# Loading and splitting weight blocks in pairs in a float32 gMLP and dilated-attention kernel

## The chip, the cores and the metric

The kernel runs on one core of a Trainium2 chip. The metric is the device time of one execution in microseconds (us), the median over several runs. The engines are called as in the profile: PE (TensorE matmul), PEld (its weight loads), DVE (VectorE), ACT (ScalarE), POOL (GpSimd) and SP (SyncE, which here issues the DMA transfers, one after the other, in the order of its program).

## What is computed

The reference is a two-layer decoder on 2048 tokens of width 1024, all in float32. Cut to its products:

```python
def gmlp_layer(x, c, ada_w, ada_b, norm_g, w_in, sgu_g, w_s, b_s, w_out):
    shift, scale, gate = ada_mod(c, ada_w, ada_b, 3)
    h = rms_norm(x, norm_g) * (1 + scale) + shift
    u, v, z = jnp.split(h @ w_in, 3, axis=-1)            # 3 x 2048 columns
    v = rms_norm(jax.nn.gelu(v), sgu_g)                  # chunks of 128 tokens, 8 groups
    mixed = einsum('gts,bcsge->bctge', tril(w_s), v) + b_s
    return x + gate * ((gelu(u) * mixed * silu(z)) @ w_out)

def shared_kv(...):        # h @ w_kv, 1536 columns; k is normalised per head
def dilated_layer(...):
    q, z = split(h @ w_in) # 3 groups of 8 heads x 128, and z with 1024 columns
    o = softmax-merge over 3 groups of banded, dilated attention(q, k, v)
    return x + gate * ((o * silu(z)) @ w_out)
```

## The kernel before

The 2048 tokens are worked on in four quarters Q = 0 to 3 of 512 tokens. In each quarter the dense products follow one another on PE: v (`dense`), u and z of the first layer (`dense_f`), its output o (`dense`), then k and v of the shared attention (kv, `dense`), and the blocks q02, q01, q00 and z0b (`dense_s`; in quarter Q the blocks q(Q)2, q(Q)1, q(Q)0, z(Q)b). The last stage, `finish`, merges the attention and multiplies by the output weights (tiles `wo`).

To keep float32 accuracy, each operand is held as a high half, rounded to the matmul type fp32r, and a low half, the remainder. A product is three matmuls: high by high, low by high, high by low. Weights come from DRAM as float32 into a tile `raw_*`; `split` makes the high half by an ACT copy (L242) and the low half by a DVE subtraction (L246), both into a tile `w_*`. The subtraction of the few blocks of `begin` and before is on POOL.

- `wunits` (called by `dense`, `dense_s` and the start, `begin`) loads blocks of 128 rows by 512 columns, 256 KB each: one DMA (L253), one ACT copy, one subtraction. `dense` takes eight such blocks in one pass of 10.9 us of PE. `dense_s` does a 1024x1024 product by seven smaller products of four blocks each (24 matmuls of 128x512 for each half of the tokens); between the products ACT and DVE empty PSUM tiles into sum tiles (`st_*`; L386 adds, L391 copies).
- `dense_f` loads blocks of 2 x 128 rows by 256 columns, 256 KB, four for one block of output columns.
- The raw tiles come from a pool `rp` of six, the `w_*` tiles from a pool `wp` of eight: a load can be issued only when the split has read the tile that it overwrites, and a split only when PE is done with the weights that it overwrites. The tiles `og` (two attention groups' output, 512 KB each) and `zt` of `finish` take places in `wp` too, three a step.
- Beside this chain run generators ("fillers"): attention of the quarter before, preparation of the operands, combined weights, the ada vectors (`aw_*` loads, `acc_*` on DVE). `tick` advances them by a rate at each k of a dense block. In the last z block (quarter 3) these are the generators of `finish`: `w_out` loads the 16 blocks of the output weights (`rawo`; L1055, ACT L1057, POOL L1058), and `first` loads og and zt (L1096, L1098), scales og on ACT (L1105, eight operations) and on DVE (L1043), adds on DVE (L1107) and multiplies by zt on POOL (L1108).
- The query blocks end in a short chain on POOL (L780 to L783), after which SP stores the rows of q (`qd<-st_q..`, L785). The z blocks end in an ACT operation (L791) and a store (`zd<-zb`, L792).

A scheduler orders the instructions of each engine when the program is built. On the chip each engine, and SP's list of transfers, runs in that order: an instruction that waits holds up all that stand behind it on its engine.

Of the kernel before, what the change touches and what calls it, by code (L numbers as in the profile page):

```python
# [12 lines left out]
F32 = mybir.dt.float32  # L13
# [21 lines left out]
def trunk(ctx, tc, out, x, c, a_ada_w, a_ada_b, a_norm_g, a_w_in, a_sgu_g, a_w_spatial,  # L35
# [9 lines left out]

    cp = ctx.enter_context(tc.tile_pool(name="cp", bufs=1))
    big = ctx.enter_context(tc.tile_pool(name="big", bufs=6))
    wp = ctx.enter_context(tc.tile_pool(name="wp", bufs=8))
    rp = ctx.enter_context(tc.tile_pool(name="rp", bufs=6))
    xp = ctx.enter_context(tc.tile_pool(name="xp", bufs=4))  # L50
    ep = ctx.enter_context(tc.tile_pool(name="ep", bufs=6))
    bp = ctx.enter_context(tc.tile_pool(name="bp", bufs=2))
# [194 lines left out]

    def wunits(w, k0, n0, nm, nk=KT, ordered=False):
        us = []
        for kk in range(nk):  # L250
            u = wp.tile([P, 2, 512], F32R, tag="w", name=f"w_{nm}{kk}")
            raw = rp.tile([P, 512], F32, tag="raw", name=f"raw_{nm}{kk}")
            ld = nc.sync.dma_start(raw, w[(k0 + kk) * P:(k0 + kk + 1) * P, n0:n0 + 512])  # L253
            if ordered:
                tc.keep_in_program_order(ld)
            split(u[:, 0, :], u[:, 1, :], raw, ordered)
            us.append(u)
        return us

    last_mm = [None]  # L260
# [24 lines left out]
    def dense_f(hh, hl, w, n0, nm, evac):  # L285

        pts = [pst(f"pd_{nm}_{i}", "d") for i in range(2)]
        for kk in range(0, KT, 4):
            for j in range(0, 4, 2):
                u = wp.tile([P, 2, 2, 256], F32R, tag="w", name=f"w_{nm}{kk + j}")  # L290
                raw = rp.tile([P, 2, 256], F32, tag="raw", name=f"raw_{nm}{kk + j}")
                nc.sync.dma_start(
                    raw, w[(kk + j) * P:(kk + j + 2) * P, n0:n0 + 256].rearrange("(k p) n -> p k n", p=P))
                split(u[:, 0], u[:, 1], raw)
                for k in (kk + j, kk + j + 1):
                    for i in range(2):
                        wh = u[:, 0, k % 2, i * P:(i + 1) * P]
                        wl = u[:, 1, k % 2, i * P:(i + 1) * P]
                        nc.tensor.matmul(pts[i], wh, hh[:, k, :], start=k == 0, stop=False)  # L299
                        nc.tensor.matmul(pts[i], wh, hl[:, k, :], start=False, stop=False)  # L300
                        nc.tensor.matmul(pts[i], wl, hh[:, k, :], start=False, stop=k == KT - 1)  # L301
                    tick(0.25)
        for i in range(2):
            evac(i, pts[i])

# [742 lines left out]
    def finish():  # L1048
        wo = {}

        def w_out(n):
            wh, wl = wo[n] = [big.tile([P, KT, 512], F32R, tag="big", name=f"wo{n}{i}") for i in range(2)]
            for kk in range(KT):
                raw = rp.tile([P, 512], F32, tag="raw", name=f"rawo{n}{kk}")
                nc.sync.dma_start(raw, b_w_out[kk * P:(kk + 1) * P, n * 512:(n + 1) * 512])  # L1055
                yield
                nc.scalar.activation(wh[:, kk, :], raw, AF.Copy)  # L1057
                nc.gpsimd.tensor_tensor(wl[:, kk, :], raw, wh[:, kk, :].bitcast(F32), ALU.subtract)  # L1058
                yield

        gb = [bcast(gd[1:2, n * 512:(n + 1) * 512], f"gb{n}") for n in range(2)]
# [29 lines left out]
        def load(t):  # L1091
            rw = slice(t * P, (t + 1) * P)
            og = {}
            for g in (0, 2):
                og[g] = wp.tile([P, D], F32, tag="w", name=f"og{t}_{g}")
                nc.sync.dma_start(og[g], od[g][rw, :])  # L1096
            og["z"] = wp.tile([P, D], F32, tag="w", name=f"zt{t}")
            nc.sync.dma_start(og["z"], zd[rw, :])  # L1098
            return og

# [140 lines left out]
```

## Time and profile before

| | |
|---|---|
| median of 3 runs | 3061.34 us (3060.43 to 3061.94) |
| profiled execution, span from first to last instruction | 3054.5 us |
| what lies around the span (median less span) | 6.8 us |
| PE busy | 2966.3 us, 97% |
| DVE busy | 2003.8 us, 66% |
| ACT busy | 1632.3 us, 53% |
| POOL busy | 835.4 us, 27% |
| DMA queue | 55% of 16 engines' time, 544.93 MB |

The profile is that of one execution. It has no time of its own besides its span; the runs' times count some microseconds around it. PE is busy nearly all the time, so the table says at once that only the 88.2 us in which PE is idle, and the stretches in which PE runs at its lower clock, can move the time down, and that each wait that is added in front of PE moves it up.

### The profile page before, as it was taken

How to read it: one execution, taken by the hardware profiler on the slowest of the kernel's cores; microseconds unless marked ns; L12 is line 12 of the kernel's file. 1: busy time of each engine (PE TensorE's matmuls, PEld its weight loads, DVE VectorE, ACT ScalarE, POOL GpSimd, SP SyncE). 2: the span in 40 equal slices, each digit the busy share in tenths (PEclk: the TensorE clock that was granted, in tenths of full speed). 3: DMA queues.
4: the chain of work that ended last, by engine and by line, in shares of the span. 5: the costliest groups of instructions: out<-in, count | busy, mean ns of one | idle time of the engine just before them, and what ended most of it. 6: DMA issues, size and time to landing. Idle time of an engine off the chain costs nothing. (4 is left out here: it accounts for less than half of the span.)

```text
span 3054.5 us, 45283 instructions
## 1 busy us (share of the span) xinstructions
PE 2966.3 (97%) x14928; PEld 2487.1 (81%) x14928; DVE 2003.8 (66%) x3550; ACT 1632.3 (53%) x3324; POOL 835.4 (27%) x1112
## 2 busy tenths in 40 slices
PE   5999999999999999999999999999999999999999
PEld 4788888788888778888888878788888888877787
DVE  6777466773567477865577386856676577768862
ACT  4323345666466245566466265566455367867540
POOL 4047113330013023523133033423222131134332
PEclk8999999999999999999999999999999999999999
DMA  7799546663433367753433366743333366778742
GB/s 235 262 296 343 178 152 199 225 227 115 153 97 114 97 201 233 233 189 119 136 101 107 106 194 210 257 152 122 122 108 112 120 192 212 230 252 287 235 153 97
DMA packets 343487, 547.82 MB, mean 179 GB/s; under 512 B 36074, under 2 KB 135628, under 8 KB 343252
## 3 DMA queue, kind: packets, MB, share of 16 engines
q1 hardware_dynamic: 343252, 544.93, 55.1%
q8 instruction: 118, 1.93, 0.3%
q14 instruction: 117, 0.96, 0.1%
HBM read 439.28 MB, written 105.52 MB: 178 GB/s over the span
## 5 line engine op out<-in xcount | busy, mean ns | idle before, releaser
L264 PE MATMUL pd_v<-w_v,hAh 128*128 128x512 f32 x1024 | 328.0, 401 | 1.2 <-ACT hAh L450 1.2
L264 PE MATMUL pd_o<-w_o,yh 128*128 128x512 f32 x1024 | 318.0, 391 | 0.0
L264 PE MATMUL pd_kv<-w_kv,hkh 128*128 128x512 f32 x768 | 241.4, 393 | 3.2 <-DVE w_kv L246 3.2
L264 PEld LDWEIGHTS pd_o<-w_o,yh 128*128 128x128 f32 x1024 | 192.8, 189 | 39.9
L264 PEld LDWEIGHTS pd_v<-w_v,hAh 128*128 128x128 f32 x1024 | 190.1, 192 | 40.2 <-issue 1.7
L933 ACT ACTIVATE pr<-pr,stat,rt 128x256 f32<-128x256 f32 (+1 forms) x320 | 177.4, 556 | 56.6 <-DVE stat L927 39.9
L299 PE MATMUL pd_u<-hAh,w_u 128*128 128x512 f32 x512 | 207.2, 405 | 0.0
L299 PE MATMUL pd_z<-hAh,w_z 128*128 128x512 f32 x512 | 204.8, 400 | 0.0
L301 PE MATMUL pd_u<-hAh,w_u 128*128 128x512 f32 x512 | 201.1, 393 | 2.3 <-DVE w_u L246 2.3
L264 PE MATMUL pd_v<-w_v,hAl 128*128 128x512 f32 x512 | 202.9, 396 | 0.0
L301 PE MATMUL pd_z<-hAh,w_z 128*128 128x512 f32 x512 | 200.5, 392 | 0.0
L264 PE MATMUL pd_o<-w_o,yl 128*128 128x512 f32 x512 | 200.3, 391 | 0.0
L300 PE MATMUL pd_u<-hAl,w_u 128*128 128x512 f32 x512 | 200.3, 391 | 0.0
L300 PE MATMUL pd_z<-hAl,w_z 128*128 128x512 f32 x512 | 199.7, 390 | 0.0
L242 ACT ACTIVATE w_o<-raw_o 128x512 fp32r<-128x512 f32 x128 | 80.0, 630 | 195.0 <-PE pd_o L264 137.3
L246 DVE TENSOR_TENSOR w_o<-raw_o,w_o 128x512 fp32r<-128x512 f32 x128 | 89.9, 704 | 134.1 <-ACT w_o L242 133.4
L264 PEld LDWEIGHTS pd_kv<-w_kv,hkh 128*128 128x128 f32 x768 | 144.1, 189 | 34.9 <-DVE w_kv L246 4.9
L242 ACT ACTIVATE w_u<-raw_u 128x512 fp32r<-128x512 f32 x128 | 79.0, 630 | 164.1 <-PE pd_u L301 70.1
L994 PEld LDWEIGHTS po<-kv,pT 128*128 128x128 f32 x1200 | 147.4, 191 | 14.3 <-POOL pT L968 3.9
L994 PE MATMUL po<-kv,pT 128*128 128x128 f32 x1200 | 150.4, 275 | 5.7 <-POOL pT L968 3.5
L941 POOL TENSOR_TENSOR dg<-pr,ident 128x256 f32<-128x256 f32 x76 | 57.4, 755 | 358.7 <-ACT pr L933 334.4
L242 ACT ACTIVATE w_z<-raw_z 128x512 fp32r<-128x512 f32 x128 | 78.4, 626 | 141.5 <-PE pd_z L301 61.1
(664 smaller groups left out, 7752.3 us busy)
## 6 DMA issues: line engine op xcount, KB each, us to landing
raw_q<-in_b_w_in_dram SPq DMA_DIRECT2D x144, 256.0 KB, 3.8
raw_v<-in_a_w_in_dram SPq DMA_DIRECT2D x128, 256.0 KB, 3.9
raw_u<-in_a_w_in_dram SPq DMA_DIRECT2D x128, 256.0 KB, 3.3
raw_z<-in_a_w_in_dram SPq DMA_DIRECT2D x128, 256.0 KB, 3.1
raw_o<-in_a_w_out_dram SPq DMA_DIRECT2D x128, 256.0 KB, 3.0
qt<-qd SPq DMA_DIRECT2D x96, 260.0 KB, 3.8
raw_kv<-in_w_kv_dram SPq DMA_DIRECT2D x96, 256.0 KB, 3.0
od<-ot SPq DMA_DIRECT2D x96, 256.0 KB, 2.6
```

The source lines that it names most:

```text
L242: nc.scalar.activation(hi, src, AF.Copy)
L246: e.tensor_tensor(lo, src, hi.bitcast(F32), ALU.subtract)
L264: last_mm[0] = nc.tensor.matmul(pt, a, u[:, w, :], start=f, stop=e, skip_group_check=more)
L299: nc.tensor.matmul(pts[i], wh, hh[:, k, :], start=k == 0, stop=False)
L300: nc.tensor.matmul(pts[i], wh, hl[:, k, :], start=False, stop=False)
L301: nc.tensor.matmul(pts[i], wl, hh[:, k, :], start=False, stop=k == KT - 1)
L933: nc.scalar.activation(pr[:, i, :], pr[:, i, :], AF.Exp, bias=mneg[:, i:i + 1], scale=u["rt"][:, h:h + 1], accum_out=lsum[:, i:i + 1])
L941: nc.gpsimd.tensor_tensor(dg, prev, ident.unsqueeze(1).broadcast_to([P, hp, P]), ALU.mult)
L994: nc.tensor.matmul(po[:, h * P:(h + 1) * P], u["pT"][h // hp][:, h % hp, j, :], u["kv"][:, j, kh, 1, :], start=j == 0, stop=j == nk - 1)
```

## The change

Weight blocks are loaded two at a time, in one DMA of 512 KB into one raw tile of 1024 columns, and split by one ACT and one DVE operation of 1024 columns into one `w_*` tile. The pools have half as many tiles of twice the size. In `dense_f` one load takes 4 x 128 rows by 256 columns. In `finish`, `w_out` loads pairs too, but still splits in operations of 512 columns; `og` takes one pair tile of `wp` (both groups in it), and `zt` takes a tile of the raw pool. The matmuls stay as they are.

```diff
-    wp = ctx.enter_context(tc.tile_pool(name="wp", bufs=8))
-    rp = ctx.enter_context(tc.tile_pool(name="rp", bufs=6))
+    wp = ctx.enter_context(tc.tile_pool(name="wp", bufs=4))
+    rp = ctx.enter_context(tc.tile_pool(name="rp", bufs=3))
...
     def wunits(w, k0, n0, nm, nk=KT, ordered=False):
         us = []
-        for kk in range(nk):
-            u = wp.tile([P, 2, 512], F32R, tag="w", name=f"w_{nm}{kk}")
-            raw = rp.tile([P, 512], F32, tag="raw", name=f"raw_{nm}{kk}")
-            ld = nc.sync.dma_start(raw, w[(k0 + kk) * P:(k0 + kk + 1) * P, n0:n0 + 512])
+        for kk in range(0, nk, 2):
+            u = wp.tile([P, 2, 2, 512], F32R, tag="w", name=f"w_{nm}{kk}")
+            raw = rp.tile([P, 2, 512], F32, tag="raw", name=f"raw_{nm}{kk}")
+            ld = nc.sync.dma_start(
+                raw, w[(k0 + kk) * P:(k0 + kk + 2) * P, n0:n0 + 512].rearrange("(k p) n -> p k n", p=P))
             if ordered:
                 tc.keep_in_program_order(ld)
-            split(u[:, 0, :], u[:, 1, :], raw, ordered)
-            us.append(u)
+            split(u[:, 0], u[:, 1], raw, ordered)
+            us += [u[:, :, i, :] for i in range(2)]
         return us
...
-            for j in range(0, 4, 2):
-                u = wp.tile([P, 2, 2, 256], F32R, tag="w", name=f"w_{nm}{kk + j}")
-                raw = rp.tile([P, 2, 256], F32, tag="raw", name=f"raw_{nm}{kk + j}")
-                nc.sync.dma_start(
-                    raw, w[(kk + j) * P:(kk + j + 2) * P, n0:n0 + 256].rearrange("(k p) n -> p k n", p=P))
-                split(u[:, 0], u[:, 1], raw)
...
+            u = wp.tile([P, 2, 4, 256], F32R, tag="w", name=f"w_{nm}{kk}")
+            raw = rp.tile([P, 4, 256], F32, tag="raw", name=f"raw_{nm}{kk}")
+            nc.sync.dma_start(
+                raw, w[kk * P:(kk + 4) * P, n0:n0 + 256].rearrange("(k p) n -> p k n", p=P))
+            split(u[:, 0], u[:, 1], raw)
...
-            for kk in range(KT):
-                raw = rp.tile([P, 512], F32, tag="raw", name=f"rawo{n}{kk}")
-                nc.sync.dma_start(raw, b_w_out[kk * P:(kk + 1) * P, n * 512:(n + 1) * 512])
+            for kk in range(0, KT, 2):
+                raw = rp.tile([P, 2, 512], F32, tag="raw", name=f"rawo{n}{kk}")
+                nc.sync.dma_start(raw, b_w_out[kk * P:(kk + 2) * P, n * 512:(n + 1) * 512]
+                                  .rearrange("(k p) n -> p k n", p=P))
                 yield
-                nc.scalar.activation(wh[:, kk, :], raw, AF.Copy)
-                nc.gpsimd.tensor_tensor(wl[:, kk, :], raw, wh[:, kk, :].bitcast(F32), ALU.subtract)
+                for i in range(2):
+                    k = kk + i
+                    nc.scalar.activation(wh[:, k, :], raw[:, i, :], AF.Copy)
+                    nc.gpsimd.tensor_tensor(wl[:, k, :], raw[:, i, :], wh[:, k, :].bitcast(F32), ALU.subtract)
+                    yield
                 yield
...
-            for g in (0, 2):
-                og[g] = wp.tile([P, D], F32, tag="w", name=f"og{t}_{g}")
+            pair = wp.tile([P, 2, D], F32, tag="w", name=f"og{t}")
+            for i, g in enumerate((0, 2)):
+                og[g] = pair[:, i, :]
                 nc.sync.dma_start(og[g], od[g][rw, :])
-            og["z"] = wp.tile([P, D], F32, tag="w", name=f"zt{t}")
+            og["z"] = rp.tile([P, D], F32, tag="raw", name=f"zt{t}")
```

The scheduler orders the instructions anew. PE's order stays nearly the same; SP has 536 transfers fewer (1980 to 1444), DVE 524 operations fewer (3552 to 3028, the low halves 1048 to 524), ACT 526 fewer (2814 to 2288). Three places matter below.

SP's transfers in the z block of quarter 3, from the time in which its second product (on weights `z3bt`) runs; `raw_z3b` are the weights of the third product, `qd<-st_q30u` the last stores of the query block, `rawo` output weights. Before:

```order
L1055 DMA rawo_25540<-in_b_w_out_dram 128x512
L253 DMA raw_z3b_0_25563<-in_b_w_in_dram 128x512
L253 DMA raw_z3b_1_25568<-in_b_w_in_dram 128x512
L1096 DMA og_0_25554<-od_95 128x1024
L1096 DMA og_2_25556<-od_97 128x1024
L785 DMA qd_92<-st_q30u_24835 128x520
L785 DMA qd_92<-st_q30u_24836 128x520
L1098 DMA zt_25558<-zd 128x1024
L253 DMA raw_z3b_2_25573<-in_b_w_in_dram 128x512
L253 DMA raw_z3b_3_25578<-in_b_w_in_dram 128x512
```

And now, with the loads of the fourth product (`raw_z3bt` from `wt_2`) behind them:

```order
L1055 DMA rawo_22948<-in_b_w_out_dram 128x2x512
L1103 DMA zt_22965<-zd 128x1024
L785 DMA qd_92<-st_q30u_22325 128x520
L1101 DMA og_22962<-od_95 128x1024
L785 DMA qd_92<-st_q30u_22326 128x520
L1101 DMA og_22962<-od_97 128x1024
L253 DMA raw_z3b_0_22970<-in_b_w_in_dram 128x2x512
L253 DMA raw_z3b_2_22975<-in_b_w_in_dram 128x2x512
L253 DMA raw_z3bt_0_23025<-wt_2_117 128x2x512
L253 DMA raw_z3bt_2_23030<-wt_2_117 128x2x512
```

The first two blocks of the third product stood ahead of both og loads and both stores of q; now all of its blocks stand behind these four. Behind these rows come two `rawo` transfers, the two stores of the third product's result (`zd<-zb`) and only then the loads of the fifth product.

DVE at the same place: the low halves of the third product's weights (`w_z3b`), and what stands around them. Before:

```order
L1043 TENSOR_TENSOR og_2_25556<-og_2_25556,wst 128x1024
L246 TENSOR_TENSOR w_z3b_0_25562<-raw_z3b_0_25563,w_z3b_0_25562 128x512
L246 TENSOR_TENSOR w_z3b_1_25567<-raw_z3b_1_25568,w_z3b_1_25567 128x512
L1107 TENSOR_TENSOR og_0_25554<-og_0_25554,og_2_25556 128x1024
L386 TENSOR_TENSOR st_z3bu_25491<-pd_z3ba_25433,st_z3bu_25491 128x512
L386 TENSOR_TENSOR st_z3bu_25492<-pd_z3ba_25434,st_z3bu_25492 128x512
L246 TENSOR_TENSOR w_z3b_2_25572<-raw_z3b_2_25573,w_z3b_2_25572 128x512
```

And now:

```order
L1043 TENSOR_TENSOR og_22962<-og_22962,wst 128x1024
L386 TENSOR_TENSOR st_z3bu_22911<-pd_z3ba_22863,st_z3bu_22911 128x512
L386 TENSOR_TENSOR st_z3bu_22912<-pd_z3ba_22864,st_z3bu_22912 128x512
L1112 TENSOR_TENSOR og_22962<-og_22962 128x1024
L246 TENSOR_TENSOR w_z3b_0_22969<-raw_z3b_0_22970,w_z3b_0_22969 128x1024
L246 TENSOR_TENSOR w_z3b_2_22974<-raw_z3b_2_22975,w_z3b_2_22974 128x1024
```

The first low half stood behind the scaling of og (L1043) alone; now the two additions of the second product's result (L386) and the addition of the og tiles (L1107, now L1112) stand ahead of it too.

SP's transfers in the first u block of quarter 0, where the loads of the ada weights (`aw_bsc`) run among the loads of u's weights. Before:

```order
L166 DMA aw_bsc_1412<-in_b_ada_w_dram 128x2x512
L292 DMA raw_u_1417<-in_a_w_in_dram 128x2x256
L166 DMA aw_bsc_1433<-in_b_ada_w_dram 128x2x512
L292 DMA raw_u_1444<-in_a_w_in_dram 128x2x256
L166 DMA aw_bsc_1460<-in_b_ada_w_dram 128x2x512
```

And now:

```order
L166 DMA aw_bsc_1317<-in_b_ada_w_dram 128x2x512
L166 DMA aw_bsc_1338<-in_b_ada_w_dram 128x2x512
L166 DMA aw_bsc_1360<-in_b_ada_w_dram 128x2x512
L292 DMA raw_u_1385<-in_a_w_in_dram 128x4x256
L292 DMA raw_u_1423<-in_a_w_in_dram 128x4x256
L292 DMA raw_u_1486<-in_a_w_in_dram 128x4x256
L166 DMA aw_bsc_1401<-in_b_ada_w_dram 128x2x512
```

One block of u for each ada load has become three blocks of twice the size in a row, and the ada loads behind them are later.

## Rows read from the trace of the kernel before

**Rows 1.** The page: the span, and the busy time of each engine.

```profile
span 3054.5 us, 45283 instructions
PE 2966.3 (97%) x14928; PEld 2487.1 (81%) x14928; DVE 2003.8 (66%) x3550; ACT 1632.3 (53%) x3324; POOL 835.4 (27%) x1112
```

**Rows 2.** Waits of PE: total us, times, longest us, by releaser.

```profile
PE pc_a L616 <- DVE acc_a L612: 24.0, 4, 17.9
...
PE pd_z3bb L264 <- ACT w_z3b L242: 4.0, 2, 3.7
...
PE pd_kv L264 <- DVE w_kv L246: 3.2, 4, 1.7
...
PE pd_u L301 <- DVE w_u L246: 2.3, 2, 1.8
...
PE pd_q00b L264 <- ACT w_q00t L242: 1.5, 1, 1.5
...
PE pd_z3bb L264 <- DVE w_z3b L246: 1.3, 3, 0.7
...
PE pd_q20b L264 <- ACT w_q20t L242: 1.0, 1, 1.0
```

**Rows 3.** Groups by line and form: busy us, mean ns | idle before, releasers.

```profile
L246 DVE TENSOR_TENSOR w_q<-raw_q,w_q 128x512 fp32r<-128x512 f32 x144 | 98.1, 700 | 36.7 <-ACT w_q L242 35.2
...
L1107 DVE TENSOR_TENSOR og<-og,og 128x1024 f32<-128x1024 f32 x16 | 19.5, 1220 | 3.3 <-ACT og L1105 2.9 <-DVE og L1043 0.2
...
L242 ACT ACTIVATE w_o<-raw_o 128x512 fp32r<-128x512 f32 x128 | 80.0, 630 | 195.0 <-PE pd_o L264 137.3 <-issue 38.1 <-PE pd_z L301 13.6
```

**Rows 4.** DMA issues: KB each, median us from issue to landing.

```profile
raw_q<-in_b_w_in_dram SPq DMA_DIRECT2D x144, 256.0 KB, 3.8
...
raw_kv<-in_w_kv_dram SPq DMA_DIRECT2D x96, 256.0 KB, 3.0
...
og<-od SPq DMA_DIRECT2D x32, 512.0 KB, 4.2
```

**Rows 5.** Timeline, PE in the last z block (start us, us, then the operation).

```profile
2717.46 5.60 PE L264 MATMUL pd_z3bb<-w_z3b,hob 128*128 128x512 f32 x24
...
2732.55 0.80 PE L264 MATMUL pd_z3bb<-w_z3b,hob 128*128 128x512 f32 x1 [3.69 <-ACT w_z3b L242]
...
2741.89 5.60 PE L264 MATMUL pd_z3ba<-w_z3bt,hob 128*128 128x512 f32 x24
...
2764.32 4.66 PE L264 MATMUL pd_z3bb<-w_z3b,hob 128*128 128x512 f32 x18 [0.36 <-ACT w_z3b L242]
```

**Rows 6.** Timeline of the same block on SP, POOL, ACT and DVE.

```profile
2723.67 0.87 SPq L253 DMA_DIRECT2D raw_z3b<-in_b_w_in_dram  x2
...
2726.79 1.29 POOL L1058 TENSOR_TENSOR wo<-rawo,wo 128x512 fp32r<-128x512 f32 x1 [4.04 <-ACT wo L1057]
...
2730.30 1.83 SPq L785 DMA_DIRECT2D qd<-st_q30u  x2
...
2736.27 2.38 POOL L1108 TENSOR_TENSOR og<-og,zt 128x1024 f32<-128x1024 f32 x1 [4.48 <-PE pd_z3bb L264]
...
2742.58 1.28 ACT L791 ACT_TABLE_LOAD   x1
```

**Rows 7.** Windows: us, busy of each engine, granted PE clock, DMA share, GB/s.

```profile
160.00:165.00 5.00, 5.00 (x22) 4.54 (x20) 3.91 (x7) 2.34 (x4) 0.00 (x0) 0.51 0.92 288
...
2730.00:2735.00 5.00, 2.10 (x4) 1.41 (x5) 2.91 (x4) 3.96 (x11) 1.55 (x4) 0.68 0.64 211
2735.00:2740.00 5.00, 4.72 (x13) 3.39 (x13) 4.05 (x5) 2.05 (x4) 2.55 (x2) 0.64 0.95 324
```

**Rows 8.** Timeline, PE in the first u block of quarter 0.

```profile
156.77 0.50 PE L301 MATMUL pd_u<-hAh,w_u 128*128 128x512 f32 x1 [1.77 <-DVE w_u L246]
```

**Rows 9.** Timeline, DVE and PE at quarter 0's first kv block, which starts at 432.73.

```profile
437.56 2.40 DVE L246 TENSOR_TENSOR w_kv<-raw_kv,w_kv 128x512 fp32r<-128x512 f32 x2
...
438.17 0.61 PE L264 MATMUL pd_kv<-w_kv,hkh 128*128 128x512 f32 x2
```

More of the change, by code (lines that the diff above doesn't have):

```diff
@@ L288, in dense_f @@
         for kk in range(0, KT, 4):
-            for j in range(0, 4, 2):
-                u = wp.tile([P, 2, 2, 256], F32R, tag="w", name=f"w_{nm}{kk + j}")
-                raw = rp.tile([P, 2, 256], F32, tag="raw", name=f"raw_{nm}{kk + j}")
-                nc.sync.dma_start(
-                    raw, w[(kk + j) * P:(kk + j + 2) * P, n0:n0 + 256].rearrange("(k p) n -> p k n", p=P))
-                split(u[:, 0], u[:, 1], raw)
[L295 to L302, printed above, removed]
+            u = wp.tile([P, 2, 4, 256], F32R, tag="w", name=f"w_{nm}{kk}")
[3 more added lines that the diff above has]
+            split(u[:, 0], u[:, 1], raw)
+            for k in range(kk, kk + 4):
+                for i in range(2):
+                    wh = u[:, 0, k % 4, i * P:(i + 1) * P]
+                    wl = u[:, 1, k % 4, i * P:(i + 1) * P]
+                    nc.tensor.matmul(pts[i], wh, hh[:, k, :], start=k == 0, stop=False)
+                    nc.tensor.matmul(pts[i], wh, hl[:, k, :], start=False, stop=False)
+                    nc.tensor.matmul(pts[i], wl, hh[:, k, :], start=False, stop=k == KT - 1)
+                tick(0.25)
         for i in range(2):
@@ L1052, in w_out @@
             wh, wl = wo[n] = [big.tile([P, KT, 512], F32R, tag="big", name=f"wo{n}{i}") for i in range(2)]
-            for kk in range(KT):
-                raw = rp.tile([P, 512], F32, tag="raw", name=f"rawo{n}{kk}")
-                nc.sync.dma_start(raw, b_w_out[kk * P:(kk + 1) * P, n * 512:(n + 1) * 512])
+            for kk in range(0, KT, 2):
+                raw = rp.tile([P, 2, 512], F32, tag="raw", name=f"rawo{n}{kk}")
+                nc.sync.dma_start(raw, b_w_out[kk * P:(kk + 2) * P, n * 512:(n + 1) * 512]
+                                  .rearrange("(k p) n -> p k n", p=P))
                 yield
-                nc.scalar.activation(wh[:, kk, :], raw, AF.Copy)
-                nc.gpsimd.tensor_tensor(wl[:, kk, :], raw, wh[:, kk, :].bitcast(F32), ALU.subtract)
+                for i in range(2):
+                    k = kk + i
+                    nc.scalar.activation(wh[:, k, :], raw[:, i, :], AF.Copy)
+                    nc.gpsimd.tensor_tensor(wl[:, k, :], raw[:, i, :], wh[:, k, :].bitcast(F32), ALU.subtract)
+                    yield
                 yield
```

## The prediction

> **What bounds the kernel now.** I read the page first. PE is busy for 2966.3 of 3054.5 us, DVE for 66% and ACT for 53% [rows 1]. So the time is PE's: 88.2 us of idle PE are all that a better order could take away, apart from stretches at the lower clock, and work saved on DVE, ACT or SP counts only where PE waits for it. The second view was therefore PE's list of waits [rows 2]. Its largest entry, 24.0 us, is for the ada sums at the start and has nothing to do with weights. The waits for a weight split add up to 4.0 + 3.2 + 2.3 + 1.5 + 1.3 + 1.0 = 13.3 us, and these six rows also name the places where the slack of the weight chain is gone: the z block of quarter 3, the kv blocks, the first u block, and q00 and q20. Everywhere else the chain has slack: ACT sits idle for 195.0 us before the o splits, 137.3 of them because PE has not yet released the weight tiles [rows 3]. There a split may become later by a few us, and nothing happens.
>
> Third, the timeline at these places. In the last z block seven products of 24 matmuls, at 5.60 us or a little less each [rows 5], ought to take about 39 us; they took from 2717.46 to 2764.32 + 4.66 = 2768.98, that is 51.5. The third product alone waits 3.69 us for its first weights [rows 5]. Then the clock falls: the granted clock was 0.68 and 0.64 in the 10 us from 2730 to 2740, which is (0.32 + 0.36) x 5 = 3.4 us lost [rows 7]. The first u block shows the same pair, a wait of 1.77 us for a split [rows 8], and then 5 us at 0.51, that is 2.45 us lost [rows 7].
>
> **What the change removes.** Two low halves of 512 columns cost 2 x 0.70 us on DVE; an operation of 1024 columns on the same types costs 1.22 [rows 3]. That is 0.18 us for each of 524 pairs, some 94 us less DVE work. ACT: two halves cost 2 x 0.63 [rows 3]. No row has ACT at 1024 columns; it lies between 0.63 (the columns cost nothing) and 1.26 (no fixed part). I take 1.16, nearest to what DVE does in proportion, and save about 0.1 x 524 = 52 us. None of this is on the path except where PE waits for splits, so I cost it at nothing; the cover is the slack named above. SP issues 536 transfers fewer; it is a queue and counts through what is late behind it.
>
> **What it adds.** A pair is ready later than its first block was. A block takes 3.0 to 3.8 us to land [rows 4], 0.63 to round, 0.70 to subtract [rows 3]: about 4.9. A pair takes 4.2 to land, if it behaves like the 512 KB loads of og [rows 4], then 1.16 and 1.22: 6.6. It can also start one block later: with eight tiles a split may run seven blocks ahead of PE, with four pairs only six. A block is six matmuls, 1.4 us [rows 5], so 1.4 + 0.53 + 0.52, about 2.4 us of slack go at every place that the weight tiles limit.
>
> On landing the Trainium skill (DMA: Bandwidth & Descriptors, § Anatomy of one DMA) gives about 2.0 us fixed plus bytes / 436 GB/s, by an estimate 2.6 us for a block and 3.2 for a pair. That is less than the trace shows for either size [rows 4]; by it the sum below would be 1 us lower, about 3070.
>
> **The z block of quarter 3.** Here a term is large. All loads of the third product now stand behind both stores of q and both og loads on SP. Before, the two stores occupied SP from 2730.30 to 2732.13, waiting for the chain on POOL, which stood behind one wo operation of 1.29 us [rows 6]. Now the second store's chain stands behind two of these, with its first steps ahead of them, so I leave its issue near 2731.5. The second og load follows at 2731.9 and the third product's first pair at about 2732.3, against 2723.67 for the first two blocks before [rows 6]. It lands 4.2 later, at 2736.5, and is rounded at 2737.7. DVE is later still: og lands at 2736.1, then come its scaling (1.22), two additions (0.70 each) and the og sum (1.22), so the low half begins at 2740.0 and ends at 2741.2. PE's second matmul needs it; before, that wait was over at 2732.55 + 0.80 + 0.34 = 2733.69 [rows 5]. **+7.5.** The clock falls after the wait as it did before, the same 3.4.
>
> The fourth product: its second pair's ACT operation now stands behind the two result operations of the third product. After that product's end come two operations of 0.63, the pair's 1.16 and 1.22: 3.6 us, needed after 12 matmuls, 2.8. **+0.8**; the table load of 1.28 [rows 6] can run before the end. The fifth product's loads stand behind the two stores of that result, and its first low half behind the fourth's additions: third product's end, two results (1.3), two stores, the load 4.2, splits 2.4 give about 8.7, and with the additions 9.0, where the fourth product ends at 0.8 + 5.6 = 6.4. **+2.6.** For sixth and seventh I take nothing more. Sum **+11**. Bounds: if stores and og come early, only DVE's order is left (second product's end, then 1.4 + 1.22 + 1.22, no later than before), so 0 + 0.8 + 2.6, about +3. At the top another clock fall, 3.4, and a late zt that keeps its raw tile until POOL's 2.38 us are done [rows 6]: +17.
>
> **The first u block.** Three loads of u's weights now stand in a row ahead of ada loads; before, each stood behind one. Of the wait of 2.3 [rows 2] and the 2.45 us at low clock behind it, I take **-3**. Bounds: -4.75 if all goes, +2 if the first, bigger load comes 2 us later than the block did.
>
> **The kv blocks, four times.** The low half of blocks 4 and 5 stands where block 5's stood, behind the additions to the residual; there DVE starts the next two at 437.56 and takes 1.20 each instead of 0.70 [rows 9]. A pair starting at 437.6 takes between 1.22 and 2.4 us, to 438.8 to 440.0. Block 4 is needed at 432.73 + 4 x 1.36 = 438.17, where PE's row stands [rows 9], its low half a matmul later. So +0.4 to +1.6 each; nearer the first, 0.8, is +3.2. Against this the second kv block of each quarter, where the four waits of 3.2 us are [rows 2], has an operation less ahead of its second pair: -2. Net **+1** (-3 to +5).
>
> **q00 and q20.** They already wait for splits, 1.5 and 1.0 us [rows 2], and lose 2.4 us of slack, but DVE and SP have fewer items ahead of them. I take **+1.5** (-2.5, both gone, to +6, the 2.4 paid there and in z0 to z2). Start and tail: the start waits for the ada sums [rows 2], and `finish` has the same depth of og and zt, four steps and three: 0.
>
> **Sum:** 11 - 3 + 1 + 1.5 = +10.5 on the profiled span: 3065.0. The median of the runs lies 6.8 us above that span, and I add the change to the median: 3061.34 + 10.5, about **3072 us**.
>
> **Rivals.** (a) *It cancels.* The stores are early, z pays +3, u0 gives 3, kv and q00 between -2 and +2: about 3062. For it: much of the third product's delay rests on one store's time. Against it: DVE's order there. (b) *It is faster.* The time that DVE, ACT and SP win reaches the places where PE waits: u0 -4.75, kv -3, q00 and q20 -2.5, z +1, so -9, 3052. It decides when the pair's low half in z is not behind a late og, that is, when og lands before 2732. For it: all six rows of waits on splits are waits for DVE or ACT, and these lose 146 us of work. Against it: pairs are later exactly at the tight places. The Trainium skill (VectorE: DVE Perf Modes, § The TRN2 errata and § Rules for kernel authors) speaks for this rival: a fixed cost per instruction, so fewer and larger ones. The trace agrees on the price, 1.22 against 1.40 [rows 3]; whether it reaches PE no page says. (c) *Three raw pairs become the limit.* A raw pair is held 4.2 + 1.16 + 1.22 = 6.6 us, so three of them give a pair each 2.2 us, against 2.8 that PE needs; a wo pair holds its tile for two POOL operations, 2.6 more. If SP also waits, q00, q20 and the four z blocks pay 2 to 3 us each, with one more clock fall: +20, 3081. Against it: 2.2 is still under 2.8 in quiet places.
>
> **Numbers.** The forecast (+6 to +16) 0.40; (c) 0.15; (a) 0.27; (b) 0.18. A run of this kernel cannot be told from no change within some 0.2%, 6.1 us. So faster by more 0.18, the same 0.27, slower 0.55. The range leaves out part of (b) and the top of (c): 3054 to 3086; the forecast's own is 3066 to 3078.
>
> **What would show it.** In the new profile PE's waits should name the third and fifth products of z3b, with 8 to 11 us for the third; SP should issue the third product's first pair after 2732 less what was gained before; the waits for w_u should shrink; w_kv waits should appear at the first kv block; a DVE pair should take 1.15 to 1.3 us, an ACT pair 1.1 to 1.2, a 512 KB load 3.5 to 4.5. I am wrong if the third product's pair is issued by 2728, if ACT takes near 0.63, or if waits for raw tiles turn up in q00 and z0 to z2.

## The result and the profile after

The changed kernel took 3087.76 us (median of 4 runs, 3084.89 to 3092.27), beside 3061.44 of the kernel before, measured with it. The ratio is 1.009, with an interval of 1.0076 to 1.0105: **slower by 0.9%, 26 us**, where 10.5 were forecast. The profiled span grew from 3054.5 to 3084.7, by 30.2 us. The profiled execution itself took 3086.45, 1.7 us more than its span, and in every later run that has both numbers the difference is 1.7 to 2.1. So the 6.8 us that the prediction took to lie around the span were mostly the difference between two executions of the kernel before.

The page, which answers to [rows 1]:

```profile
span 3084.7 us, 42215 instructions
PE 2972.7 (96%) x14928; PEld 2488.1 (81%) x14928; DVE 1932.8 (63%) x3026; ACT 1553.8 (50%) x2798; POOL 862.1 (28%) x1108
```

DVE lost 71 us of work and ACT 79 us, as the change promises, and the kernel is slower. PE is busy 6 us longer, at a mean granted clock of 0.991 after 0.994, and idle 24 us longer. The list of PE's waits says for what, and answers to [rows 2]:

```profile
PE pd_z3bb L265 <- ACT w_z3b L242: 13.4, 2, 12.9
...
PE pd_z3bb L265 <- ACT w_z3bt L242: 3.2, 1, 3.2
...
PE pd_z0ba L265 <- DVE st_z0bu L386: 2.4, 1, 2.4
PE pd_z3bb L265 <- DVE w_z3b L246: 2.1, 3, 1.1
PE pd_q20a L265 <- DVE w_q L246: 2.0, 1, 2.0
PE pd_q00a L265 <- DVE w_q L246: 2.0, 1, 2.0
...
PE pd_z0ba L265 <- DVE w_z0bt L246: 1.5, 1, 1.5
...
PE pd_q12b L265 <- DVE w_q12t L246: 1.4, 1, 1.4
```

The waits for w_u and w_kv of [rows 2] are gone, 2.3 and 3.2 us. In their place stand waits in q and z blocks of every quarter, each short, and one of 12.9 us in the last z block (`pd_` and `st_` are the PSUM and sum tiles of a block, so a wait for `st_z0bu L386` is one for DVE's addition).

To see where the 30 us came in, take the start of the first matmul of each block in both profiles, and the difference of each stretch between two such starts. All columns but the first are differences to the kernel before, in us; the other kernels are the experiments below. "q, z" are the blocks from the first q to z of that quarter, with the second kv block; "v to o" are the four first-layer blocks; "kv" is the first kv block, all four quarters summed.

| stretch | before | changed | all_single | late_og | b_rp5 | b_rp4 | a_e5t7 | rp4_e5t7 |
|---|---|---|---|---|---|---|---|---|
| v, u of quarter 0 | 228.1 | -8.5 | -2.4 | -6.8 | -2.3 | -4.9 | -6.4 | -8.1 |
| first kv blocks, all four | 194.5 | -3.3 | +2.0 | -3.3 | +0.4 | +7.8 | +0.5 | +0.4 |
| q, z of quarter 0 | 182.1 | +8.2 | +7.0 | +9.1 | +6.1 | +17.6 | +7.4 | -3.1 |
| q, z of quarter 1 | 179.6 | +7.6 | +5.2 | +6.6 | +8.4 | +27.6 | +3.0 | +1.4 |
| q, z of quarter 2 | 180.5 | +3.0 | +2.6 | +2.4 | +2.9 | +16.8 | +2.9 | -2.1 |
| v to o of quarters 1 to 3 | 1309.8 | +8.0 | -0.1 | +2.0 | -2.5 | +3.7 | +10.6 | +2.5 |
| q of quarter 3 | 238.2 | +1.3 | +1.2 | +2.4 | +0.2 | +2.5 | +4.1 | +2.6 |
| last z block | 51.5 | +15.9 | +12.5 | +5.5 | +10.0 | +14.2 | +14.5 | +1.5 |
| tail | 285.5 | -2.3 | -1.2 | +0.4 | -0.3 | +0.8 | -1.7 | -1.8 |
| span | 3054.5 | +30.2 | +27.0 | +18.3 | +23.1 | +85.3 | +35.1 | -6.3 |

(The start and the z and o blocks of quarter 0 differ by less than 1 us and are left out.) Single executions differ by a few us, also where the order of the instructions is the same: q, z of quarter 1 by 4.6 between the changed kernel and a_e5t7, the summed row v to o by 6.0 between the changed kernel and late_og. One fall of the clock costs some 3 us (2.45 and 3.4 in the two stretches of [rows 7]). So a difference of up to 5 us in one row says little.

Of the 18.8 us in the q and z blocks of quarters 0 to 2, 10.2 are idle PE (5.2 before, 15.4 now) and 8.5 longer busy time; the granted clock of the three stretches is 0.98, 1.00 and 0.99, after 1.00 in each.

**The last z block.** Its timeline on SP, ACT, POOL, DVE and PE, which answers to [rows 5, 6]; the block now starts at 2733.99:

```profile
2744.09 0.38 SPq L1055 DMA_DIRECT2D rawo<-in_b_w_out_dram  x1
...
2749.28 1.15 ACT L1060 ACTIVATE wo<-rawo 128x512 fp32r<-128x512 f32 x2 [7.04 <-DMA rawo<-in_b_w_out_dram]
...
2751.36 1.26 POOL L1061 TENSOR_TENSOR wo<-rawo,wo 128x512 fp32r<-128x512 f32 x1
...
2752.80 0.32 SPq L785 DMA_DIRECT2D qd<-st_q30u  x1
2753.18 0.42 SPq L1101 DMA_DIRECT2D og<-od  x1
2753.69 0.92 SPq L253 DMA_DIRECT2D raw_z3b<-in_b_w_in_dram  x2
...
2759.55 1.22 PE L265 MATMUL pd_z3bb<-w_z3b,hob 128*128 128x512 f32 x2 [12.87 <-ACT w_z3b L242]
...
2760.62 4.52 DVE L246 TENSOR_TENSOR w_z3b<-raw_z3b,w_z3b 128x1024 fp32r<-128x1024 f32 x2
```

Read it upwards from PE: the wait of 12.87 us ends with a weight pair that SP issued at 2753.69, behind an og load, behind a store of q, which waited for POOL, which did two wo operations first, which waited for a load of 5.2 us. That is the chain of the prediction, link by link; the issue is 4.9 us later than it was priced. DVE's two low halves then take 2.3 us each, where the median is 1.22, with POOL's og operation beside them.

**A q and a z block.** Timeline of DVE, SP and PE in q00's third product, and of SP, DVE and PE in z0:

```profile
570.87 0.38 SPq L253 DMA_DIRECT2D raw_q<-in_b_w_in_dram  x1
...
572.61 1.22 DVE L246 TENSOR_TENSOR w_q00t<-raw_q00t,w_q00t 128x1024 fp32r<-128x1024 f32 x1
...
574.19 2.67 SPq L785 DMA_DIRECT2D qd<-st_q01w  x2
...
576.96 0.68 SPq L253 DMA_DIRECT2D raw_q<-in_b_w_in_dram  x1
...
581.25 1.06 ACT L242 ACTIVATE w_q<-raw_q 128x1024 fp32r<-128x1024 f32 x1 [3.64 <-DMA raw_q<-in_b_w_in_dram]
...
584.53 0.17 DVE L892 COPY rt<-qt 128x8 f32<-128x8 f32 x1 [4.72 <-DMA qt<-qd]
584.70 1.23 DVE L246 TENSOR_TENSOR w_q<-raw_q,w_q 128x1024 fp32r<-128x1024 f32 x1
...
585.99 3.86 PE L265 MATMUL pd_q00a<-w_q,hob 128*128 128x512 f32 x11 [2.02 <-DVE w_q L246]
```
```profile
613.71 0.93 SPq L253 DMA_DIRECT2D raw_z0bt<-wt  x2
619.25 0.81 SPq L785 DMA_DIRECT2D qd<-st_q00w  x2
620.16 1.04 SPq L253 DMA_DIRECT2D raw_z0b<-in_b_w_in_dram  x2
620.72 1.28 DVE L386 TENSOR_TENSOR st_q00u<-pd_q00a,st_q00u 128x512 f32<-128x512 f32 x2
...
624.00 2.21 DVE L246 TENSOR_TENSOR w_z0bt<-raw_z0bt,w_z0bt 128x1024 fp32r<-128x1024 f32 x1
...
626.27 2.80 PE L265 MATMUL pd_z0ba<-w_z0bt,hob 128*128 128x512 f32 x11 [1.52 <-DVE w_z0bt L246]
```

A raw pair is held from its load's issue to the end of its one subtraction. The pair of q00 is held from 576.96 to 585.93, 9.0 us, and the second of the two of z0 from about 614.2 to 626.2, 12 us. In between the subtraction stands behind a copy that waits for a load of the attention (q00), or behind PSUM additions and the operations after them (z0, where the subtraction itself takes 2.21). These two are among the longer: over the 153 pairs that are loaded in the q and z blocks of quarters 0 to 2, the mean from issue to end of subtraction is 8.8 us. Divided by three tiles that is a pair each 2.9 us, and PE needs one in 2.8.

The short ring also acts through SP's order. By the order of the loads, the one at 570.87 took the raw tile that DVE had released at 570.84. The one at 576.96 had a tile from 573.83 on (572.61 and 1.22), but stands in SP's list behind two stores of q, which waited for POOL; with a fourth pair, below, the scheduler puts it ahead of them.

The prices themselves came out near the forecast. A group each of DVE and ACT, and three loads, to compare with [rows 3, 4]:

```profile
L246 DVE TENSOR_TENSOR w_o<-raw_o,w_o 128x1024 fp32r<-128x1024 f32 x64 | 79.7, 1245 | 141.1 <-ACT w_o L242 140.8
L242 ACT ACTIVATE w_o<-raw_o 128x1024 fp32r<-128x1024 f32 x64 | 67.8, 1059 | 151.9 <-PE pd_o L265 102.1 <-issue 47.3 <-PE pd_z L301 2.1
```
```profile
raw_q<-in_b_w_in_dram SPq DMA_DIRECT2D x72, 512.0 KB, 4.5
raw_v<-in_a_w_in_dram SPq DMA_DIRECT2D x64, 512.0 KB, 6.2
...
raw_o<-in_a_w_out_dram SPq DMA_DIRECT2D x64, 512.0 KB, 3.5
```

### The profile page after: what moved, and what is told of

Its sections match the earlier page's. It is cut to its first block, busy times and chain, and to the rows that moved or that the text cites. A ratio compares the mean times of both kernels' runs of the same rounds, so it can differ in the third digit from the quotient of the medians.

```text
span 3084.7 us, 42215 instructions
## 1 busy us (share of the span) xinstructions
PE 2972.7 (96%) x14928; PEld 2488.1 (81%) x14928; DVE 1932.8 (63%) x3026; ACT 1553.8 (50%) x2798; POOL 862.1 (28%) x1108
## 5 line engine op out<-in xcount | busy, mean ns | idle before, releaser
L246 DVE TENSOR_TENSOR w_o<-raw_o,w_o 128x1024 fp32r<-128x1024 f32 x64 | 79.7, 1245 | 141.1 <-ACT w_o L242 140.8
L994 PEld LDWEIGHTS po<-kv,pT 128*128 128x128 f32 x1200 | 147.4, 192 | 14.2 <-POOL pT L968 4.4
L923 DVE SCALAR_TENSOR_TENSOR pr<-dist,rt,ps 128x256 f32<-128x256 f32 (+1 forms) x320 | 122.8, 430 | 45.1 <-PE ps L920 27.1
L265 PE MATMUL pd_kv<-w_kv,hkl 128*128 128x512 f32 x384 | 150.9, 393 | 0.0
L242 ACT ACTIVATE w_o<-raw_o 128x1024 fp32r<-128x1024 f32 x64 | 67.8, 1059 | 151.9 <-PE pd_o L265 102.1
```

Of the source, the lines that this page charges most:

```text
L242: nc.scalar.activation(hi, src, AF.Copy)
L246: e.tensor_tensor(lo, src, hi.bitcast(F32), ALU.subtract)
L265: last_mm[0] = nc.tensor.matmul(pt, a, u[:, w, :], start=f, stop=e, skip_group_check=more)
L923: nc.vector.scalar_tensor_tensor(pr[:, i, :], dist[:, 256 - w:256], u["rt"][:, h:h + 1], psc[:, i, :], ALU.mult, ALU.add)
L994: nc.tensor.matmul(po[:, h * P:(h + 1) * P], u["pT"][h // hp][:, h % hp, j, :], u["kv"][:, j, kh, 1, :], start=j == 0, stop=j == nk - 1)
```

## The experiments

Theories ahead of the first runs: (A) the pairs' coarse operations come late in the seven-product blocks and stand behind waiting items; (B) the rings are in effect shallower, because a pair tile comes free only when both halves are done with; (C) finish's own edits, og in one pair tile and zt in a raw tile, make the last block's loss. Each run stands against the kernel before on its own chip, 3055.6 to 3057.1 us there.

**s_single and all_single**: coarse operations taken back, tiles left in pairs. In `wunits`, for the four-block calls (s_single) or for all but the start's ordered loads, and in `dense_f` too (all_single):

```diff
+            lds = [nc.sync.dma_start(raw[:, i, :], w[(k0 + kk + i) * P:(k0 + kk + i + 1) * P, n0:n0 + 512])
+                   for i in range(2)]
...
+            for i in range(2):
+                split(u[:, 0, i, :], u[:, 1, i, :], raw[:, i, :], ordered)
```

> Pair tiles and halved pools as in the changed kernel, but in the seven-product blocks (dense_s) each half of a pair is loaded and split by an operation of its own; dense and dense_f stay in pairs. Theory A (the loss is in dense_s and comes from the coarse operations: a pair's load and split come later and stand behind waiting items on SP and DVE): the losses of the q and z blocks, some +8 in quarter 0, +8 in quarter 1, +3 in quarter 2 and +16 in the last z block, mostly go, the gain of 8 in the first u block stays: 3052 to 3064 us. Theory B (tiles come free in pairs only, so the rings are in effect shallower): 3080 to 3092. Theory C (finish: zt in a raw tile, og in one pair tile): the last z block keeps its +16, the others recover: 3066 to 3076.

Measured 3087.69 us, ratio 1.0103 (1.0086 to 1.0119): the q and z blocks of quarters 0 to 2 lose 23.9 us together (changed kernel: 18.8), the last z block 9.7.

> Pair tiles and halved pools, but every load and every split is of one block as before (only the start's ordered loads stay in pairs); what is left of the change is that tiles come free in pairs, and finish. Theory A: 3055 to 3068, near the kernel before, without the gain in the first u block. Theory B: 3080 to 3100. Theory C: about 3072 to 3080, the loss in the last z block alone.

Measured 3085.88 us, 1.0098 (1.008 to 1.0116). With every load and split of one block again the loss is nearly whole, so theory A falls as the main cause. C, which has the loss in the last z block alone, does not explain the 14.8 us in the q and z blocks of quarters 0 to 2. B remains. One row differs: "v to o" is back at -0.1, while s_single, with pairs in `dense`, has +3.1.

**dma_pair and split_pair**: loads in pairs and splits single, and the reverse.

```diff
+            for i in range(2):
+                split(u[:, 0, i, :], u[:, 1, i, :], raw[:, i, :], ordered)   # dma_pair, below one load of 512 KB
...
+            split(u[:, 0], u[:, 1], raw, ordered)                            # split_pair, below two loads of 256 KB
```

> Loads in pairs, splits of single blocks, pair tiles. If the late landing and the place of the 512 KB loads on SP are the cost (A1): 3080 to 3092, as the changed kernel. If the 1024-column splits and what stands behind them on DVE and ACT are the cost (A2): 3055 to 3068.

Measured 3102.35 us, 1.0149 (1.0129 to 1.017).

> Loads of single blocks, splits in pairs, pair tiles. A1 (loads are the cost): 3055 to 3068. A2 (splits are the cost): 3080 to 3092; a pair's split then waits for two loads, so its waits should read DMA raw before ACT in the z blocks.

Measured 3081.99 us, 1.0086 (1.0068 to 1.0104). Neither half recovers; both expectations of a recovery missed. A load of a pair with single splits is worst (q and z of quarters 0 to 2: +36.7); single loads with one split (+14.2) cannot be told from the changed kernel. Theory B alone does not give this order: in dma_pair the raw pairs of these blocks are held 8.5 us in the mean, no longer than the 8.8 of the changed kernel. Why it is worst stays open.

**late_og**: only the place of the og and zt loads in the last z block, and with it that of the operations on og.

```diff
             yield from weights(0, NT - TPQ)
+            for _ in range(8):
+                yield
             ogs[0] = load(0)
```

> The changed kernel with one edit: the generator that loads the first og and zt waits eight more of its turns, so that these loads stand behind the weights of the third to fifth product of the last z block, and the third product's weights stand ahead of or between the two q stores. If that block's loss of 16 us is the place of its loads on SP: the third product's wait of 12.9 us falls to 0 to 3, the block to between +2 and +6 of the kernel before, the time by 10 to 14 us to 3073 to 3079. If the raw ring itself is too short there: the block stays above +10.

Measured 3079.00 us, 1.0069 (1.0052 to 1.0085), the last z block +5.5: both at the upper end of what was expected for the place of the loads, and PE's wait above it. Its SP and PE rows:

```profile
2739.26 0.46 SPq L253 DMA_DIRECT2D raw_z3b<-in_b_w_in_dram  x1
2740.27 0.34 SPq L785 DMA_DIRECT2D qd<-st_q30u  x1
2740.71 0.37 SPq L253 DMA_DIRECT2D raw_z3b<-in_b_w_in_dram  x1
...
2746.31 0.79 PE L265 MATMUL pd_z3bb<-w_z3b,hob 128*128 128x512 f32 x1 [4.96 <-ACT w_z3b L242]
```

With the pair ahead of the store, og out of the way, PE waits 4.96 where it waited 12.87. So with three raw pairs, the place of the og and zt loads, with the operations that hang on them, makes about two thirds of this block's loss, and none of the 19 us in the q and z blocks.

**zt_wp**: zt back in the weight pool.

```diff
-            og["z"] = rp.tile([P, D], F32, tag="raw", name=f"zt{t}")
+            og["z"] = wp.tile([P, 2, D], F32, tag="w", name=f"zt{t}")[:, 0, :]
```

> The changed kernel with zt in a tile of the weight pool again, so that it takes no raw tile. The third product's first pair is then loaded ahead of the last two q stores, its second pair still behind them and og. Theory C (zt in the raw ring makes the loss): the last z block to +5 or less, time 3074 to 3080. If the order of the other items decides: the second pair waits instead, block +8 to +13, time 3080 to 3088. In the tail the weight pool is shorter by one step, which may cost up to 5 us.

Measured 3104.96 us, 1.0155 (1.0139 to 1.0172): last z block +12.4, tail +15.0. The tail's price was three times what I allowed. So zt in a raw tile is not what makes most of the last block's loss.

**raw_ring**: the raw tiles as six single places in one tile, each overwritten as soon as its own split has read it; four-block calls and wo single.

```diff
+    rring = rp.tile([P, 6, 512], F32, name="rring")
...
+                raw = rslots(n)      # n = 1 in dense_s and w_out, 2 elsewhere
```

> Raw tiles as a ring of six single places again, each free as soon as its own split has read it: dense_s and the output weights load and split single blocks, dense and dense_f pairs; the weight tiles stay four pairs, zt is in the weight pool. Theory B for the raw ring: the blocks q00 to z2 lose less than 5 us in all, z3 at most 6, time 3060 to 3068. Theory B for the weight tiles (free in pairs only): the blocks q00 to z2 still lose 10 to 18 us, time 3075 to 3090.

Measured 3088.11 us, 1.0097 (1.008 to 1.0114). The last z block is at +4.7, as expected, the q and z blocks at +13.5, and the tail at +16.2, because zt had to be in the weight pool. The expectation for weight tiles that come free in pairs, 10 to 18 us in these blocks, is met. Against s_single, which splits in the same pieces, the single raw places give back 10 of 24 us; the rest is with the weight pairs or with the order that the scheduler made. So by this run the raw ring is part of the loss, and not shown to be all of it.

**b_rp4, b_rp5 and b_wp6**: the kernel before, all single, with one pool cut.

```diff
-    rp = ctx.enter_context(tc.tile_pool(name="rp", bufs=6))
+    rp = ctx.enter_context(tc.tile_pool(name="rp", bufs=5))    # b_rp5; 4 in b_rp4; wp 8 to 6 in b_wp6
```

> The kernel before with one edit: four raw tiles instead of six, all else single as it was. Three pair tiles of which one is half read are worth four to five single tiles. If the depth of the raw ring is what the pairs cost: losses at the same places, q00 to z2 together +6 to +15, z3 +5 to +12, time 3068 to 3080. If not: 3055 to 3064.

Measured 3142.24 us, 1.028 (1.0261 to 1.0299): q and z of quarters 0 to 2 lose 62.0 us, four times the upper end of what I expected.

> The kernel before with five raw tiles instead of six, all single. If three pair tiles are worth about five single ones because both halves stay until the pair's split has read them: the q and z blocks of quarters 0 to 2 lose 12 to 25 us, the last z block 7 to 15, time 3075 to 3095. If the step from six to five costs little and only four is too few: under 3066.

Measured 3082.37 us, 1.0094 (1.0076 to 1.0112). One raw tile fewer in the kernel before, and nothing else but the order that the scheduler makes for it (in the q and z blocks of quarters 0 to 2 it moves 51 of 504 transfers, 13 of 647 DVE and 2 of 584 ACT operations): q and z +17.4 (changed kernel +18.8), the last z block +10.0. Its waits of PE are in the same blocks, but mostly for PSUM additions:

```profile
PE pd_z3bb L264 <- ACT w_z3b L242: 7.0, 2, 4.8
...
PE pd_q10b L264 <- DVE st_q10u L386: 4.1, 1, 4.1
...
PE pd_z0ba L264 <- DVE st_z0bu L386: 2.5, 2, 2.0
...
PE pd_q00a L264 <- ACT st_q00u L391: 2.0, 1, 2.0
```

> The kernel before with six weight tiles instead of eight, six raw tiles. If the weight tiles' depth matters as the raw ring's does: q and z blocks of quarters 0 to 2 lose over 10 us. If the raw ring alone matters: they lose under 5 us; the tail may lose up to 15, since og and zt take weight tiles there and one step fewer fits.

Measured 3102.94 us, 1.0154 (1.0134 to 1.0174), but at other places: first kv blocks +18.1 together, 2 to 3 us in each of three o blocks, the last z block +7.4; q and z of quarters 0 to 2 lose 8.0, between what the two expectations have. The changed kernel does not lose at the kv blocks (-3.3). Its pattern is that of the kernel with a short raw ring, not of the one with few weight tiles.

**b_late and ring_f_late**: can the kernel before be improved by the same means? b_late is the edit of late_og; ring_f_late has the raw ring, single weight tiles, `dense_f` with one load of 512 KB and two splits, and that edit.

> The kernel before with the first og and zt loads eight turns later, as in late_og: all four weights of the last z block's third product then stand ahead of the q stores. If the place of the loads on SP makes the 13 us that this block loses already before the change: the block 5 to 11 us shorter, the time 3046 to 3053 where the kernel before takes 3057. If not: within 2 us of it.

Measured 3063.86 us, 1.0024 (1.0013 to 1.0035). The block is 1.2 us longer, not 5 to 11 shorter: with six raw tiles it waits next for the additions to PSUM (3.8 us for L386), and the tail loses 7.8. A miss.

> A version put together from what the runs show: single weight tiles and splits as before, raw tiles as a ring of six places, each free by itself, only dense_f loads in pairs (one DMA of 512 KB, two splits), and og and zt eight turns later. If the first u block's gain of 6 us comes from the paired loads: u block -4 to -7, last z block -4 to -10, kv unchanged, time 3042 to 3052. If it comes from the paired DVE operations: u block within 2, time 3047 to 3055.

Measured 3060.91 us, 1.0024 (1.0013 to 1.0034). The first u block is 4.6 us shorter, but b_late, with that stretch untouched, had 2.0 too; the tail loses 8.1. Not better than the kernel before.

**rp4_e5t7, with a_e5t7 and b_e5t7 as controls**: the repair. A fourth raw pair needs 4 KB a partition, which come from two other pools; each control has these two pools alone.

```diff
-    rp = ctx.enter_context(tc.tile_pool(name="rp", bufs=3))
+    rp = ctx.enter_context(tc.tile_pool(name="rp", bufs=4))
-    ep = ctx.enter_context(tc.tile_pool(name="ep", bufs=6))
+    ep = ctx.enter_context(tc.tile_pool(name="ep", bufs=5))
-    tp = ctx.enter_context(tc.tile_pool(name="tp", bufs=8))
+    tp = ctx.enter_context(tc.tile_pool(name="tp", bufs=7))
```

> Control for the next run: the changed kernel with one tile fewer in two other pools (ep five instead of six, tp seven instead of eight), which frees the 4 KB a partition that a fourth raw pair needs. It takes what the changed kernel takes, or a few us more: 3086 to 3100.

Measured 3090.40 us, 1.0108 (1.0093 to 1.0123).

> The same with a fourth raw pair tile, everything in pairs as in the changed kernel. If the raw ring's depth makes the loss (as five and four single tiles did in the kernel before): the blocks q00 to z2 lose 12 us or more less than in the control, the last z block 5 to 10 less, time 15 to 28 under the control, 3062 to 3080. If pairs lose by being coarse whatever the depth: within 6 us of the control.

Measured **3049.94 us**, 0.998 (0.9968 to 0.9991): 40 us under its control, more than expected, and ahead of the kernel before, by 3 to 10 us as the interval has it. Everything is in pairs as in the changed kernel, and the q and z blocks are at -3.8, the last z block at +1.5. The largest waits for weights that are left in q and z blocks:

```profile
PE pd_z3bb L265 <- ACT w_z3b L242: 5.2, 2, 2.8
...
PE pd_z3bb L265 <- ACT w_z3bt L242: 1.7, 1, 1.7
...
PE pd_q10a L265 <- DVE w_q L246: 1.2, 1, 1.2
```

And in q00 SP issues both pairs of the third product at once, where the changed kernel had them at 570.87 and 576.96 (q00 starts at 570.29 here, at 569.97 there):

```profile
568.96 1.95 SPq L253 DMA_DIRECT2D raw_q<-in_b_w_in_dram  x2
...
582.88 0.17 DVE L892 COPY rt<-qt 128x8 f32<-128x8 f32 x1 [3.42 <-DMA qt<-qd]
583.06 1.23 DVE L246 TENSOR_TENSOR w_q<-raw_q,w_q 128x1024 fp32r<-128x1024 f32 x1
```

The copy that waits for the attention's load still stands ahead of the subtraction, but the subtraction now comes 1.6 us earlier, and PE's wait of 2.02 for it is not in the list.

This pair of runs also settles whether another order of the engines' work made the loss. Between a_e5t7 and rp4_e5t7, in the q and z blocks of quarters 0 to 2, PE's, ACT's and POOL's order is the same and 1 of 466 DVE operations stands elsewhere; only SP's list differs, in 45 of 323 transfers. There the loss goes from 13.3 to -3.8 by the fourth raw pair and the earlier loads that it allows, with the weight tiles still in four pairs. The pairs' tiles are held longer now, 10.9 us in the mean, because they are loaded earlier: divided by four that is 2.7. In the kernel before a single block is held 8.1, divided by six 1.35, and PE needs one in 1.4. So the hold time alone does not show whether a ring is too short; the runs with one tile more or fewer do.

> Control for the kernel before, with the same two pools one tile shorter: 3057 to 3070. It says what the two pools cost by themselves, and so whether pairs with four raw tiles are behind or ahead of single blocks at equal room.

Measured 3055.39 us, 0.9995 (0.9984 to 1.0006). The two pools cost nothing that can be told. It is no control of equal raw room: four pairs take 16 KB a partition, the six single tiles here 12. The kernel before with eight single raw tiles was not run, so it is not shown how much of the lead of rp4_e5t7 comes from the pairs and how much from the room.

> Four raw pairs and the first og and zt loads eight turns later. If the two causes are separate (ring depth in all q and z blocks, place of the loads in the last): the last z block at +5 or less against the kernel before, time 3 to 8 us under the run with four raw pairs alone. If the depth alone made both: no difference beyond 3 us.

Measured **3047.62 us**, 0.9964 (0.9948 to 0.9981), the lowest median of all. The last z block goes from +1.5 to -2.2, but the tail from -1.8 to +3.7, and the span is the same (3048.5 against 3048.2); the intervals of the two overlap, so it is not shown to be faster than rp4_e5t7.

## Why the prediction was wrong

The sign was right, and so was the mechanism of the last z block, but 10.5 us were forecast and 26 measured, outside the range (its upper end was 3086).

- **The failed step is "q00 and q20", with what rejected rival (c).** I gave +1.5, at most +6, to the q and z blocks, which lost 8.2, 7.6 and 3.0 us in the three quarters, 18.8 in all. I had the mechanism in rival (c), three raw pairs as the limit, at +20, and turned it down with one line: a pair is held 6.6 us, so three of them give a pair each 2.2 us, and PE needs one in 2.8. Those 6.6 us were the sum of bare durations. The trace has 8.8 in the mean, 9.0 in the pair of q00 and 12 in one of z0, since a tile is free only at the end of the subtraction, and this stands in DVE's order behind whatever waits there. Three tiles then give a pair each 2.9 us, not 2.2. That quotient alone would not prove it, but b_rp5 shows that the kernel before, too, had not one raw tile to spare, and rp4_e5t7 that the loss goes with a fourth pair. The term was worked out from the slack of the weight tiles, 2.4 us less, and took nothing for the raw tiles. Waits for raw tiles in q00 and z0 to z2 were the prediction's last sign of being wrong; PE's waits for late splits turned up there, and rival (c) with its 3081 was nearest to what was measured.
- **The last z block** was mechanism right and size off: +15.9 where +11 was forecast, within its bounds of +3 to +17. The third product is the term that was mis-sized: its second matmul starts at 2761.89, by the block's new start 11.7 later than the 2733.69 before, where +7.5 was forecast. SP issued the third product's pair at 2753.69; moved to the new start of the block (16.5 later), the forecast said 2748.8. The missing 4.9 us: the wo pair ahead took 5.2 to land among og and zt, and POOL's two operations came behind it. The order on DVE came as forecast, and the fifth product waited 3.2 for the 2.6 forecast. What I did not see is that this too hangs on the raw ring: with a fourth pair the block is at +1.5.
- **The first u block** gave more than forecast, -6.1, and v before it -2.4; the term was -3, its bound -4.75. **The kv blocks** gave -3.3 where I had +1: the pair of blocks 4 and 5 did not make PE wait, and the second pair's wait went. For kv this is rival (b)'s sense: with paired splits in `dense` (s_single, split_pair, late_og) the row is at -3.2 to -3.3 as well, with single ones (all_single, dma_pair) at +2.0 and +2.7. Only in a_e5t7 and rp4_e5t7, paired too, one wait for w_kv of 1.9 us is left. For u it is not shown: dma_pair with single splits has -6.1, split_pair with single loads -5.4, and b_e5t7 with neither -3.6.
- **v to o of quarters 1 to 3**, +8.0, had no term. It is there in kernels that split in pairs in `dense` (s_single +3.1, split_pair +1.1, a_e5t7 +10.6) and not in all_single or dma_pair (-0.1, -2.5). But late_og has the changed kernel's order in these blocks and only +2.0, and b_late the order of the kernel before and -5.3. So most of it can be the difference of single executions; the cause stays open.
- **Prices**: DVE 1.22 at the median (mean 1.24 to 1.38) for 1.22 forecast, ACT 1.06 for 1.16 (in proportion to DVE it would have been 1.10), a 512 KB load 3.5 to 6.2 us for 4.2. The slowest are v's loads, in blocks with a DMA share of 0.40 to 0.72, the fastest o's, at 0.33 to 0.35; what makes the difference is not shown. The fit of the Trainium skill (DMA: Bandwidth & Descriptors, § Anatomy of one DMA), by which I had estimated 3.2 us, is given there for transfers issued by GpSimd, and here SP issues them; it is below every one of these medians, and the measurement decides. The page of the Trainium skill on VectorE (VectorE: DVE Perf Modes, § The TRN2 errata) says that one large tile pays a fixed cost once and many small ones pay it each, and 1.22 for a pair against 2 x 0.70 agrees. That the saved work reaches PE is shown at the kv blocks alone.
- **What lies around the span** is 1.7 us, not 6.8; as the sum was made on the span's change, it moves nothing.

## What to carry to other kernels

Halving the number of buffers and doubling their size is not neutral even at equal bytes: a buffer is held from the issue of its load to the end of the last operation that reads it, waits in the reading engine's order included. Take the hold time for a forecast from a trace and not from a sum of bare durations (8.8 us here, not 6.6). But a ring that is always in use has a hold time as long as the ring allows (10.9 with four pairs, at no loss), so the measure of slack is a run: before a change of granularity, cut the pool by one in the kernel as it is. If that costs time, 26 us here, there is no slack for coarser pieces; here one more pair was worth 40 us. Where a single queue issues everything, look at what a load now stands behind, at the one place where something in that queue waits for a slow chain.

## What the runs showed that I had not expected

One raw tile of 256 KB decides 26 us (3082.37 against 3055.9), two decide 86 (3142.24 against 3056.72), in a kernel whose DMA queue is 55% and whose DVE is 66% busy. Moving the og and zt loads back gains 10 us in the last z block with three raw pairs (late_og), and nothing with six single tiles (b_late). And 536 transfers and 1050 operations fewer did not pay with three raw pairs. With four, in more room than before, the kernel is 7 us ahead (3049.94 against 3057.09), and it is not shown that this comes from the operations saved.
